# Gate/up tiles of four FFNs: all by seven block products, on operands taken from the residual stream without its reciprocal norm, and the biases of the second mixer prepared in the first

## The chip, the cores and the metric

One core of one Trainium2 chip runs the whole program. The metric is the device time of one execution in microseconds. TensorE (PE) multiplies, VectorE (DVE) and ScalarE (ACT) do the elementwise work, GpSimd (POOL) some more of it, and SyncE (SP) issues most transfers.

## The reference, cut to what matters

Two transformer blocks of two layers each run one after the other on 512 tokens (the second block adds 16 meta tokens, so 528) with 1024 features. Every layer is a mixer (four kinds, A to D) and then an FFN. What the change touches is the FFN:

```python
h = rmsnorm(x, norm_ffn[i])          # x * rsqrt(mean(x*x) + eps) * g
gu = h @ w_gate_up[i]                # 1024 -> 2 x 2816
x = x + (silu(gu[..., :D_FF]) * gu[..., D_FF:]) @ w_down[i]
```

In the second block the gate passes a causal convolution of width 3 over the tokens before the silu. The reciprocal norm is one number per token, so it can be multiplied in before the matrix product or after it.

## The kernel before, in words

Activations are kept transposed: X is eight tiles of 128 features by T tokens. Every float32 operand of a product is split into a high part, rounded to what one pass of TensorE takes, and the rest (`split`, L427: one ACT instruction, one DVE instruction), and each product is three matmuls (`mm3`, L253): hi by hi, hi by lo, lo by hi. So each weight tile costs ACT and DVE work as well as PE work.

A scheduler orders the instructions of each engine when the program is built; it follows the program's order but lets a later instruction go first where its inputs are there and an earlier one's are not. Buffers bound how far it runs ahead: 4 raw weight tiles, 4 `hi` and 4 `lo` tiles (`NRAW`, `NHI`), 3 PSUM banks for `mm`, 5 work tiles (`wk`), 60 slots.

**The norm** (`Norm`, L512) is spread over the mixer's output projection. When a tile X[k] is finished, `add` (L520) makes its operand xh, xl (L508 on ACT, L509 on DVE: X times the gain g, without the reciprocal norm) and adds its squares to `acc` (L533, L543). `sums` (L546) later reduces `acc` with small matmuls and a chain of 13 tiny DVE instructions, `rows` (L571) turns the result into a tile `rs` that holds the reciprocal norm of each token on all partitions.

**The FFN** (`ffn`, L982) runs over 22 tiles f of 128 gate and 128 up columns, in groups of 4, 2, 4, 4, 4, 4 (`GROUPS`). After a group, its share of the down product is left as a generator (`down`, L1028: eight tiles j, each added to X[j] on DVE at L687), and the next group's tiles draw on it: one down tile inside each gate/up tile (`between`), the rest behind it. During the first group there is no down work.

*Ordinary tiles*, f below 5 (`NPLAIN`): gate and up are each eight k-steps of three matmuls on xh, xl (`linT`, L266), 48 matmuls of 512 columns, or 96 of 264 with T of 528. The result is scaled by `rs` when it leaves PSUM (`scaled`, L402). Behind f = 0 to 3 stands the making of the block operands `xb` (L1024): X times gain times `rs` on DVE (`normed`, L992), then `Blocks.first` and `second` (L342, L353), with three subtractions on POOL and five splits for each of four pairs of tiles.

*Block tiles*, f from 5 on: `seven` (L294) loads the four blocks of the gate/up weights, makes four sums on DVE (L306 to L309) and splits all seven operands (three splits of 1024, one of 512). `blocks_to` (L379) computes gate and up by seven products (of 4 k-steps, 12 matmuls of 256 columns, 84 in all; 264 or 258 columns in the third and fourth FFN) and combines them with three ACT copies, three DVE additions and one more ACT copy (L400). No scaling: `xb` holds it already.

Behind either kind come the convolution (L977 on ACT, twice L980 on DVE; second block only), silu on ACT (L1022), gate times up (L1043) and its split (`ah`, `al`).

**The biases of mixer B** (`load_biases`, L1209) are prepared in the first FFN: POOL zeroes a scratch in DRAM and writes eight pieces into it (L1214, L1220), SP issues 16 DRAM-to-DRAM transfers (L1224), three at once and then one for each f from 4 on (`mid`), and at last 6 loads into SBUF and 5 of the memory keys and values (L1230, L897).

Of the kernel before, what the change touches and what calls it, by code (L numbers as in the profile page):

```python
# [9 lines left out]
F32 = mybir.dt.float32  # L10
# [24 lines left out]
NPLAIN = 5  # L35
XBAT = {0: (0,), 1: (1,), 2: (2,), 3: (3,)}
# [86 lines left out]
def kernel(ctx: ExitStack, tc: tile.TileContext, stop=None, **a):  # L123
# [170 lines left out]
    def seven(w, k0, nk, cols):  # L294
# [30 lines left out]
    class Blocks:  # L325


        def __init__(self, nk, o, n, tag, eng):
            self.n, self.o, self.tag, self.eng = n, o, tag, eng
            self.ops = {i: [None] * nk for i in range(1, 8)}  # L330
            self.raw = [None] * nk
# [7 lines left out]
        def win(self, z):  # L339
            return z[:, self.o:self.o + 2 * self.n].rearrange("p (i c) -> p i c", i=2)  # L340

        def first(self, k, z):  # L342

            h, l = slot(self.tag), slot(self.tag)
            v = self.win(z)
            split(self.part(h, 0), self.part(l, 0), v[:, 0, :])
            self.eng.tensor_tensor(v[:, 0, :], v[:, 1, :], v[:, 0, :], ALU.subtract)
            split(self.part(h, 1), self.part(l, 1), v[:, 0, :])
            for i, key in enumerate((1, 5)):
                self.ops[key][k] = self.part(h, i), self.part(l, i)  # L350
            self.raw[k] = v

        def second(self, k, z):  # L353

            v, t = self.win(z), self.raw[k]
            h, l = slot(self.tag), slot(self.tag)
            split(self.both(h), self.both(l), v)
            for i, key in enumerate((2, 3)):
                self.ops[key][k] = self.part(h, i), self.part(l, i)
            self.eng.tensor_tensor(t, v[:, 1, :].unsqueeze(1).to_broadcast([P, 2, self.n]), t, ALU.subtract)  # L360
            h, l = slot(self.tag), slot(self.tag)
            split(self.both(h), self.both(l), t)
            for i, key in enumerate((6, 7)):
                self.ops[key][k] = self.part(h, i), self.part(l, i)
            self.eng.tensor_tensor(v[:, 0, :], v[:, 0, :], t[:, 0, :], ALU.subtract)
            h = slot(self.tag)
            split(self.part(h, 0), self.part(h, 1), v[:, 0, :])
            self.ops[4][k] = self.part(h, 0), self.part(h, 1)
# [10 lines left out]
    def blocks_to(ws, bl, c1, c2, between):  # L379


        n = bl.n
# [16 lines left out]
        product(pa, 4, ws, bl, more=True)  # L399
        A.copy(c21, pa[:, :n])  # L400
# [111 lines left out]
    class Norm:  # L512
# [469 lines left out]
    def ffn(X, T, nj, wgu, wd, taps, done, lo=0, mid=None):  # L982

        xs = nj.xs
        lg = max(0, lo - 2)
        w = slice(lo, T)
        lb = max(0, lo - 4)
        xb = Blocks(4, lb, (T - lb) // 2, "xb", G)

        def normed(k, rs):  # L990
            z = wk("xn")
            V.scalar_tensor_tensor(z[:, :T], X[k][:, :T], gcol(nj.key, k), rs[:, :T], ALU.mult, ALU.mult)  # L992
            return z

        state = {}

        def up(f, put, between):
            c = f * P
            if mid is not None and f >= MID:
                next(mid, None)  # L1000
            gt, ut = wk("gt"), wk("ut")
            if f < NPLAIN:
                pcs = [wcols(wgu, 4 * h, [(c, P), (DFF + c, P)]) for h in range(2)]
                if f == 0:
                    hg, hu = Held(gt), Held(ut)
                    run(linT(pcs, 0, xs, T, hg.take, lo=lg, wide=True))
                    nj.sums()
                    run(linT(pcs, 1, xs, T, hu.take, lo=lo))
                    state["rs"] = nj.rows()
                    hg.scale(state["rs"])  # L1010
                    hu.scale(state["rs"])
# [26 lines left out]
        for gi, (f0, fn) in enumerate(GROUPS):  # L1038
# [39 lines left out]
    mnat = load_rows_of(a["mem"][0], NMEM)  # L1078


    def layer_a(X):
# [53 lines left out]
        class PairA(Pair):  # L1135
# [34 lines left out]
            def pv(self, b):  # L1170
# [3 lines left out]
                for u in range(u0, u1, P):  # L1174
# [8 lines left out]
        fill = Fill(q_tiles([6, 9, 7, 10], [3, 4]), q_tiles([2, 5, 8, 11], [2, 5]), memory_kv(),  # L1183
                    q_tiles([20, 21, 22, 23], [6, 7]))
# [6 lines left out]
    nf = Norm(S, ("norm_ffn", 0), "rsFA")  # L1191
# [15 lines left out]
    TB = []  # L1207

    def load_biases():  # L1209

        sc = dp.tile([P, 288], F32, name="rpbs")
        z = slot("zpad")[:, :288]
        G.memset(z, 0.0)
        G.dma_start(sc, z)  # L1214

        def scap(off, dims):
            return bass.AP(tensor=sc.tensor, offset=sc.offset + off, ap=dims)

        for r in range(8):
            G.dma_start(scap(r * 4608 + 8, [[384, 12], [48, 8], [1, 31]]), a["rpb_b"][0, :, 7 - r:15 - r, :])  # L1220

        td = dp.tile([P, 6 * 512], F32, name="TBd")
        for cc in range(16):
            nc.sync.dma_start(td[8 * cc:8 * cc + 8, :].rearrange("p (i j) -> p i j", j=32),  # L1224
                              scap(15 - cc, [[4608, 8], [48, 96], [1, 32]]))
            if cc > 1:
                yield
# [985 lines left out]
```

## Time and profile before

| | |
|---|---|
| runs | 2470.08, 2470.57, 2476.79 us; median 2470.57 |
| profiled execution | 2472.3 us, its span 2470.6 us |
| PE busy | 98% of the span |
| DVE, ACT, POOL busy | 73%, 48%, 9% |
| FFN gate/up of f = 0 to 4 begins at | 237.4, 814.6, 1524.2, 2106.3 us |

The profiled execution's time is its span and 1.7 us around it. Matmuls overlap, so the busy time of PE is no measure of its work: the distance from one start to the next is. A DVE instruction, too, is listed with a duration that overlaps the next one's by a little.

### The profile page before, as it was taken

The numbers are of one execution on the slowest core, as the hardware profiler recorded it, in microseconds if no ns is written. First come the engines' busy times: TensorE is split into PE (matmuls) and PEld (weight loads), VectorE is DVE, ScalarE is ACT, GpSimd is POOL, SyncE is SP. The second block draws the span as 40 slices with busy tenths as digits, with TensorE's granted clock in tenths as the row PEclk, the third lists the DMA queues.
The fourth block names the chain that finished last, engine by engine and source line by source line (L and its number), as shares of the span: only waits on it lengthen the run. The fifth ranks groups of instructions, "written<-read, shape, count | busy, mean of one in ns | idle before, by whom it ended". The sixth has DMA issues, their size and how long they took to land.

```text
span 2470.6 us, 44131 instructions
## 1 busy us (share of the span) xinstructions
PE 2428.9 (98%) x17446; PEld 2195.4 (89%) x17446; DVE 1812.7 (73%) x3531; ACT 1185.9 (48%) x2175; POOL 232.4 (9%) x359
## 2 busy tenths in 40 slices
PE   7999999999999999999999999999999999999999
PEld 6787789998887889998989999899999988989998
DVE  6875767777775778777766656888886775788885
ACT  4764435444565445445432233445444664445543
POOL 3120300003130100001011110200000000200000
PEclk9999999999999999999999999999999999999999
DMA  6152234444222223333411123123334222223332
GB/s 189 52 141 82 77 83 113 116 145 145 86 74 78 77 86 107 103 102 101 130 44 52 35 83 91 56 86 107 98 95 142 58 57 75 69 83 109 99 98 82
DMA packets 345443, 229.17 MB, mean 93 GB/s; under 512 B 54435, under 2 KB 335444, under 8 KB 345236
## 3 DMA queue, kind: packets, MB, share of 16 engines
q1 hardware_dynamic: 342212, 217.55, 30.0%
q0 software_dynamic: 2864, 8.77, 1.2%
q8 instruction: 137, 2.24, 0.4%
q14 instruction: 70, 0.57, 0.1%
q10 hardware_dynamic: 160, 0.04, 0.0%
HBM read 214.10 MB, written 13.74 MB: 92 GB/s over the span
## 4 chain that ended last, share of the span: by engine, by line
PE 83%; DVE 10%; issue 3%; ACT 2%; POOL 1%; SPq 1%; DMA 1%; DVEq 0%; ACTq 0%; POOLq 0%
PE mm L254 19%; PE mm L256 19%; PE mm L255 19%; PE pss L254 3%; PE pss L256 3%; PE pss L255 3%; DVE lo L430 2%; PE pso L254 1%; PE pso L256 1%; PE pso L255 1%; PE pss L847 1%; DVE xb L430 1%; PE pso L808 1%; PE pss L848 1%; PE pso L2045 1%
## 5 line engine op out<-in xcount | busy, mean ns | idle before, releaser
L429 ACT ACTIVATE hi<-raw 128x1024 fp32r<-128x1024 f32 (+1 forms) x454 | 470.7, 1039 | 520.5 <-PE pss L255 245.5
L430 DVE TENSOR_TENSOR lo<-raw,hi 128x1024 fp32r<-128x1024 f32 (+1 forms) x454 | 550.6, 1215 | 131.7 <-ACT hi L429 130.8
L254 PE MATMUL mm<-xh,hi 128*128 128x264 f32 (+3 forms) x1256 | 413.2, 329 | 8.0 <-ACT xh L508 2.4
L255 PE MATMUL mm<-xl,hi 128*128 128x264 f32 (+3 forms) x1256 | 405.3, 323 | 1.3 <-DVE xl L509 1.2
L256 PE MATMUL mm<-xh,lo 128*128 128x264 f32 (+3 forms) x1256 | 404.6, 323 | 0.0
L254 PE MATMUL mm<-ah,hi 128*128 128x512 f32 (+1 forms) x880 | 308.8, 352 | 7.5 <-DVE ut L404 4.9
L256 PE MATMUL mm<-xb,lo 128*128 128x256 f32 (+2 forms) x1088 | 308.1, 283 | 4.2 <-DVE lo L430 4.2
L255 PE MATMUL mm<-al,hi 128*128 128x512 f32 (+1 forms) x880 | 307.9, 350 | 0.1
L256 PE MATMUL mm<-ah,lo 128*128 128x512 f32 (+1 forms) x880 | 307.7, 350 | 0.0
L254 PE MATMUL mm<-xb,hi 128*128 128x256 f32 (+2 forms) x1088 | 307.3, 282 | 0.0
L255 PE MATMUL mm<-xb,hi 128*128 128x256 f32 (+2 forms) x1088 | 306.9, 282 | 0.0
L254 PEld LDWEIGHTS mm<-xh,hi 128*128 128x128 f32 x1256 | 238.8, 190 | 32.7 <-issue 6.7
L255 PEld LDWEIGHTS mm<-xl,hi 128*128 128x128 f32 x1256 | 238.9, 190 | 18.6 <-DVE xl L509 2.7
L256 PEld LDWEIGHTS mm<-xh,lo 128*128 128x128 f32 x1256 | 238.4, 190 | 18.4 <-issue 0.5
L687 DVE TENSOR_TENSOR xr<-mm,xr 128x512 f32<-128x512 f32 (+1 forms) x288 | 158.1, 558 | 124.1 <-PE mm L256 123.9
L256 PEld LDWEIGHTS mm<-xb,lo 128*128 128x128 f32 x1088 | 205.6, 189 | 5.1 <-DVE lo L430 5.0
L254 PEld LDWEIGHTS mm<-xb,hi 128*128 128x128 f32 x1088 | 205.5, 189 | 3.1 <-ACT hi L429 0.7
L255 PEld LDWEIGHTS mm<-xb,hi 128*128 128x128 f32 x1088 | 205.5, 189 | 2.2
L254 PEld LDWEIGHTS mm<-ah,hi 128*128 128x128 f32 x880 | 165.5, 188 | 29.8 <-DVE ut L404 6.6
L256 PEld LDWEIGHTS mm<-ah,lo 128*128 128x128 f32 x880 | 165.5, 188 | 22.7
L255 PEld LDWEIGHTS mm<-al,hi 128*128 128x128 f32 x880 | 165.5, 188 | 18.9 <-DVE al L430 1.1
L254 PE MATMUL pss<-xb,hi 128*128 128x256 f32 (+2 forms) x544 | 154.6, 284 | 0.0
(526 smaller groups left out, 5041.4 us busy)
## 6 DMA issues: line engine op xcount, KB each, us to landing
raw<-in_w_gate_up_dram SPq DMA_DIRECT2D x142, 256.0 KB, 3.0
raw<-in_ffn_w_up_dram SPq DMA_DIRECT2D x142, 256.0 KB, 3.0
raw<-in_w_down_dram SPq DMA_DIRECT2D x40, 512.0 KB, 3.4
raw<-in_ffn_w_down_dram SPq DMA_DIRECT2D x40, 512.0 KB, 3.4
raw<-in_mix_w_in_dram SPq DMA_DIRECT2D x28, 512.0 KB, 3.8
raw<-in_w_in_b_dram SPq DMA_DIRECT2D x20, 512.0 KB, 3.8
a<-in_w_gate_up_dram SPq DMA_DIRECT2D x34, 256.0 KB, 3.4
a<-in_ffn_w_up_dram SPq DMA_DIRECT2D x34, 256.0 KB, 2.9
```

The source lines that it names most:

```text
L254: PE.matmul(ps, r32(hi), r32(xh), start=first, stop=False, skip_group_check=more)
L255: PE.matmul(ps, r32(hi), r32(xl), start=False, stop=False, skip_group_check=more)
L256: PE.matmul(ps, r32(lo), r32(xh), start=False, stop=last, skip_group_check=more)
L429: A.activation(r32(dst_h), src, AF.Copy)
L430: V.tensor_tensor(r32(dst_l), src, dst_h, ALU.subtract)
L687: V.tensor_tensor(X[j][:, o:o + n], ps[:, :n], X[j][:, o:o + n], ALU.add)
L808: PE.matmul(po[64 * hh:64 * hh + 64, b * P:(b + 1) * P], self.vals(b, j, h), pt[:, (2 * hh + j) * P:(2 * hh + j + 1) * P], start=j == 0, s ...
L847: PE.matmul(ps[:, :n], r32(q), r32(k[0][:, k0:k0 + n]), start=True, stop=False)
L848: PE.matmul(ps[:, :n], r32(q), r32(k[1][:, k0:k0 + n]), start=False, stop=True)
L2045: PE.matmul(po[64 * hh:64 * hh + 64, b * P:(b + 1) * P], vt[b + j][:, kv * 64:kv * 64 + 64], PT[:, (2 * hh + j) * P:(2 * hh + j + 1) * P], ...
```

## The change

`NormB` replaces `Norm` for the four FFN norms: as each X[k] is finished in the mixer's output projection, it also makes the block operands, from X times gain without the reciprocal norm. Products 1, 2 and 3 use halves of xh, xl themselves; to make that possible, `seven` and `Blocks` now pair even with odd 128-row pieces of the contraction in place of the first four with the last four. All 22 tiles f are block tiles. `blocks_to` scales gate and up by `rs` on DVE: two more instructions and one that takes the place of the ACT copy. In f = 0 `sums` runs between products 2 and 6, and `rows` behind product 3. The biases go into the fill work of mixer A, in three pieces; their loads into SBUF are issued from POOL's queue behind the last gate/up tile of the first FFN.

```diff
-NPLAIN = 5
-XBAT = {0: (0,), 1: (1,), 2: (2,), 3: (3,)}
-    def seven(w, k0, nk, cols):
+    def seven(w, cols, nk=4):
...
-            r = (k0 + k * nk) * P
-            nc.sync.dma_start(chunks(t), w[r:r + nk * P, c:c + P].rearrange("(c p) n -> p c n", p=P))
+            nc.sync.dma_start(chunks(t), w[:, c:c + P].rearrange("(c i p) n -> i p c n", i=2, p=P)[k])
...
-        def first(self, k, z):
...
-        def second(self, k, z):
...
+        def even(self, k, x, g, xs):
+
+            self.ops[1][k] = self.half(xs, 0)
+            z = self.z = wk("xn")
+            A.activation(self.both(z), x[:, self.o:self.o + 2 * self.n].rearrange("p (i c) -> p i c", i=2), AF.Copy,
+                         scale=g)
+            z0, z1 = self.part(z, 0), self.part(z, 1)
+            V.tensor_tensor(z0, z1, z0, ALU.subtract)
+            h, l = self.t12 = slot("bt"), slot("bt")
+            split(self.part(h, 0), self.part(l, 0), z0)
+            self.ops[5][k] = self.part(h, 0), self.part(l, 0)
+
+        def odd(self, k, x, g, xs):
+
+            self.ops[2][k], self.ops[3][k] = self.half(xs, 0), self.half(xs, 1)
+            x1, x2 = self.half((x,), 0)[0], self.half((x,), 1)[0]
+            z = self.z
+            z0, z1 = self.part(z, 0), self.part(z, 1)
+            V.scalar_tensor_tensor(self.both(z), x2.unsqueeze(1).to_broadcast([P, 2, self.n]), g, self.both(z),
+                                   ALU.mult, ALU.subtract)
+            (h, l), (h2, l2) = self.t12, (slot("bt"), slot("bt"))
+            for i, (src, th, tl, j) in {6: (z0, h, l, 1), 7: (z1, h2, l2, 0), 4: (z0, h2, l2, 1)}.items():
+                if i == 4:
+                    V.scalar_tensor_tensor(z0, x1, g, z0, ALU.mult, ALU.subtract)
+                split(self.part(th, j), self.part(tl, j), src)
+                self.ops[i][k] = self.part(th, j), self.part(tl, j)
...
-    def blocks_to(ws, bl, c1, c2, between):
+    def blocks_to(ws, bl, c1, c2, rs, between, early=None, late=None):
...
         product(pd, 5, ws, bl)
+        product(pb, 2, ws, bl)
+        V.tensor_tensor(c11, pb[:, :n], p1, ALU.add)
+        if early:
+            early()
         product(pa, 6, ws, bl, more=True)
         A.copy(u2, pa[:, :n])
-        product(pb, 2, ws, bl)
-        V.tensor_tensor(c11, pb[:, :n], p1, ALU.add)
         product(pa, 7, ws, bl, more=True)
         A.copy(u3, pa[:, :n])
         V.tensor_tensor(c22, pd[:, :n], u3, ALU.add)
+        if rs is not None:
+            V.tensor_tensor(c22, c22, rs[:, w2], ALU.mult)
         between()
         product(pd, 3, ws, bl, more=True)
         V.tensor_tensor(c12, pd[:, :n], u2, ALU.add)
+        if late:
+            rs = late()
+            V.tensor_tensor(c22, c22, rs[:, w2], ALU.mult)
+        w = slice(bl.o, bl.o + 2 * n)
+        V.tensor_tensor(c1[:, w], c1[:, w], rs[:, w], ALU.mult)
         product(pa, 4, ws, bl, more=True)
-        A.copy(c21, pa[:, :n])
+        V.tensor_tensor(c21, pa[:, :n], rs[:, w1], ALU.mult)
+        return rs
...
+    class NormB(Norm):
...
+        def add(self, x):
+            k = len(self.xs)
+            Norm.add(self, x)
+            (self.bl.odd if k % 2 else self.bl.even)(k // 2, x, gcol(self.key, k), self.xs[k])
...
         def up(f, put, between):
...
-            else:
-                ws = seven(wgu, 0, 4, (c, DFF + c))
-                blocks_to(ws, xb, gt, ut, between)
+            ws = seven(wgu, (c, DFF + c))
+            state["rs"] = blocks_to(ws, xb, gt, ut, state["rs"], between, *(() if f else (nj.sums, nj.rows)))
...
-            for k in XBAT.get(f, ()):
-                xb.first(k, normed(k, state["rs"]))
-                xb.second(k, normed(k + 4, state["rs"]))
...
+        if mid is not None:
+            mid()
         run(before)
...
-        fill = Fill(q_tiles([6, 9, 7, 10], [3, 4]), q_tiles([2, 5, 8, 11], [2, 5]), memory_kv(),
-                    q_tiles([20, 21, 22, 23], [6, 7]))
+        fill = Fill(biases_out(), q_tiles([6, 9, 7, 10], [3, 4]), q_tiles([2, 5, 8, 11], [2, 5]),
+                    biases_columns(0, 8), memory_kv(), biases_columns(8, 16), q_tiles([20, 21, 22, 23], [6, 7]))
...
+    def biases_back():
         for hp in range(6):
             TB.append(slot("TB"))
-            nc.sync.dma_start(TB[hp][:, :512], td[:, hp * 512:(hp + 1) * 512])
-        memory_back()
+            G.dma_start(TB[hp][:, :512], rel["td"][:, hp * 512:(hp + 1) * 512])
+        memory_back(G)
```

`biases_out` holds the memset, the zeroing transfer and the eight writes of `load_biases` (POOL, unchanged), `biases_columns` the 16 transfers that SP issues, eight at a time. The four norms of the FFNs are now `NormB`.

## Rows read from the trace of the kernel before

**Rows 1.** The page: busy time, share and instructions of two engines; the chain by engine.
```profile
PE 2428.9 (98%) x17446; PEld 2195.4 (89%) x17446; DVE 1812.7 (73%) x3531; ACT 1185.9 (48%) x2175; POOL 232.4 (9%) x359
PE 83%; DVE 10%; issue 3%; ACT 2%; POOL 1%; SPq 1%; DMA 1%; DVEq 0%; ACTq 0%; POOLq 0%
```
**Rows 2.** Windows of ordinary tiles f = 1 to 4 and of five block products, FFN 1 to 4.
```profile
core 0: us, PE busy (x) PEld busy (x) DVE busy (x) ACT busy (x) POOL busy (x), PEclk, DMA share, GB/s
249.74:293.94 44.20, 44.20 (x195) 36.12 (x194) 36.73 (x52) 20.62 (x34) 12.15 (x10) 1.00 0.25 75
884.07:891.19 7.12, 7.12 (x61) 7.11 (x60) 4.98 (x9) 3.50 (x5) 0.00 (x0) 1.00 0.27 77
1538.30:1587.89 49.59, 47.65 (x386) 47.17 (x385) 45.73 (x70) 22.99 (x40) 13.77 (x11) 1.00 0.23 70
1603.66:1610.95 7.29, 7.29 (x62) 7.29 (x61) 4.00 (x7) 3.52 (x5) 0.00 (x0) 1.00 0.20 57
2119.91:2165.02 45.11, 45.11 (x290) 40.80 (x289) 41.13 (x60) 21.80 (x36) 13.62 (x9) 1.00 0.25 77
2178.45:2185.68 7.23, 7.23 (x61) 7.22 (x60) 5.98 (x9) 3.48 (x5) 0.00 (x0) 1.00 0.16 48
```
**Rows 3.** Windows of f = 6 to 9 in FFN 1 to 4.
```profile
327.92:387.17 59.25, 54.93 (x391) 51.20 (x389) 43.56 (x65) 28.04 (x46) 0.00 (x0) 0.97 0.34 92
905.07:956.42 51.35, 51.35 (x385) 48.55 (x384) 40.09 (x60) 26.52 (x43) 0.00 (x0) 1.00 0.33 98
1625.58:1678.22 52.64, 52.64 (x432) 52.34 (x431) 43.61 (x73) 27.48 (x45) 0.00 (x0) 1.00 0.32 96
2199.69:2251.45 51.76, 51.76 (x386) 49.48 (x384) 43.71 (x66) 28.42 (x46) 0.00 (x0) 1.00 0.33 98
```
**Rows 4.** FFN 1: a window inside f = 7; timeline of SP and of DVE (start, length).
```profile
340.00:352.00 12.00, 9.31 (x55) 8.29 (x55) 8.49 (x12) 5.91 (x10) 0.00 (x0) 0.86 0.31 88
...
307.45 3.74 SPq L1224 DMA_DIRECT2D TBd<-rpbs  x5
...
344.51 3.49 DVE L430 TENSOR_TENSOR lo<-raw,hi 128x1024 fp32r<-128x1024 f32 x3
```
**Rows 5.** DVE's group of one 256-column addition: count, busy us, mean ns.
```profile
L392 DVE TENSOR_TENSOR gt<-pso,u 128x256 f32<-128x256 f32 x34 | 14.4, 423 | 12.8 <-PE pso L256 12.7
```
**Rows 6.** Timeline of DVE, instructions one behind the other: start, length.
```profile
919.39 1.22 DVE L430 TENSOR_TENSOR lo<-raw,hi 128x1024 fp32r<-128x1024 f32 x1
920.52 0.69 DVE L430 TENSOR_TENSOR al<-ut,ah 128x512 fp32r<-128x512 f32 x1
921.13 0.68 DVE L430 TENSOR_TENSOR lo<-a,hi 128x512 fp32r<-128x512 f32 x1
...
1509.29 0.76 DVE L509 SCALAR_TENSOR_TENSOR xl<-xr,ncol,xh 128x528 fp32r<-128x528 f32 x1
1509.96 0.43 DVE L687 TENSOR_TENSOR xr<-mm,xr 128x264 f32<-128x264 f32 x1
1510.31 0.70 DVE L543 TENSOR_TENSOR acc<-acc,sq 128x528 f32<-128x528 f32 x1
```
**Rows 7.** Windows: the ends of mixers A, C and D, output projection alone.
```profile
204.00:237.40 33.40, 33.40 (x146) 27.14 (x145) 20.54 (x27) 14.76 (x20) 0.00 (x0) 1.00 0.32 94
1500.60:1524.25 23.65, 23.65 (x196) 23.65 (x195) 19.02 (x33) 12.82 (x18) 0.00 (x0) 1.00 0.31 90
2066.00:2106.20 40.20, 40.15 (x329) 39.95 (x328) 22.48 (x36) 16.36 (x22) 0.00 (x0) 1.00 0.30 87
```
**Rows 8.** DVE's timeline: first and last of the 14 instructions of the norm's chain.
```profile
243.96 0.16 DVE L457 TENSOR_SCALAR ms<-pss 128x4 f32<-128x4 f32 x1 [2.92 <-PE pss L454]
...
246.34 0.43 DVE L473 COPY rb<-rsFA 128x512 f32<-128x512 f32 x1
```
**Rows 9.** DMA issues of the biases (KB each, us to landing); a window of mixer A.
```profile
TBd<-rpbs SPq DMA_DIRECT2D x16, 96.0 KB, 3.1
...
90.00:150.00 60.00, 59.41 (x450) 48.69 (x449) 49.52 (x146) 45.33 (x120) 10.92 (x15) 1.00 0.17 54
```

More of the change, by code (lines that the diff above doesn't have):

```diff
@@ L325, with __init__, half @@
     class Blocks:
[L328 to L331, printed above, removed]
+        def __init__(self, o, n):
+            self.n, self.o = n, o
+            self.ops = {i: [None] * 4 for i in range(1, 8)}
+        def half(self, xs, i):
+            c = slice(self.o + i * self.n, self.o + (i + 1) * self.n)
+            return tuple(t[:, c] for t in xs)
         def part(self, t, i):
@@ L353, in second @@
-        def second(self, k, z):
[L355 to L368, printed above, removed]
+        def even(self, k, x, g, xs):
[8 more added lines that the diff above has]
+            self.ops[5][k] = self.part(h, 0), self.part(l, 0)
@@ L980, in conv, with ffn @@
             V.scalar_tensor_tensor(out[:, o:T], src[:, o - d:T - d], taps[n - 1 - d], out[:, o:T], ALU.mult, ALU.add)
-    def ffn(X, T, nj, wgu, wd, taps, done, lo=0, mid=None):
-        xs = nj.xs
-        lg = max(0, lo - 2)
+    def ffn(X, T, nj, wgu, wd, taps, done, mid=None, lo=0):
         w = slice(lo, T)
[L987 to L995, printed above, removed]
+        xb = nj.bl
+        state = {"rs": None}
         def up(f, put, between):
             c = f * P
-            if mid is not None and f >= MID:
-                next(mid, None)
             gt, ut = wk("gt"), wk("ut")
[L1002 to L1011, printed above, removed]
-                else:
-                    run(linT(pcs, 0, xs, T, lambda out: scaled(out, state["rs"], gt), lo=lg))
-                    run(linT(pcs, 1, xs, T, lambda out: scaled(out, state["rs"], ut), lo=lo))
-            else:
-                ws = seven(wgu, 0, 4, (c, DFF + c))
-                blocks_to(ws, xb, gt, ut, between)
+            ws = seven(wgu, (c, DFF + c))
+            state["rs"] = blocks_to(ws, xb, gt, ut, state["rs"], between, *(() if f else (nj.sums, nj.rows)))
             if taps is not None:
@@ L1078, with scap, biases_out, biases_columns @@
     mnat = load_rows_of(a["mem"][0], NMEM)
+    TB, rel = [], {}
+    def scap(off, dims):
+        return bass.AP(tensor=rel["sc"].tensor, offset=rel["sc"].offset + off, ap=dims)
+    def biases_out():
+        rel["sc"] = dp.tile([P, 288], F32, name="rpbs")
+        z = slot("zpad")[:, :288]
+        G.memset(z, 0.0)
+        G.dma_start(rel["sc"], z)
+        for r in range(8):
+            G.dma_start(scap(r * 4608 + 8, [[384, 12], [48, 8], [1, 31]]), a["rpb_b"][0, :, 7 - r:15 - r, :])
+        yield 0.1
+    def biases_columns(lo, hi):
+        if lo == 0:
+            rel["td"] = dp.tile([P, 6 * 512], F32, name="TBd")
+        for cc in range(lo, hi):
+            nc.sync.dma_start(rel["td"][8 * cc:8 * cc + 8, :].rearrange("p (i j) -> p i j", j=32),
+                              scap(15 - cc, [[4608, 8], [48, 96], [1, 32]]))
+        yield 0.1
     def layer_a(X):
@@ L1205, in to_cols @@
         lag.put(XB[j])
[L1207 to L1227, printed above, removed]
+    def biases_back():
         for hp in range(6):
             TB.append(slot("TB"))
-            nc.sync.dma_start(TB[hp][:, :512], td[:, hp * 512:(hp + 1) * 512])
-        memory_back()
+            G.dma_start(TB[hp][:, :512], rel["td"][:, hp * 512:(hp + 1) * 512])
+        memory_back(G)
     nb = Norm(S, ("norm_mix", 1), "rsB")
     lag = Lag(nb, NLAG)
-    ffn(X, S, nf, a["w_gate_up"][0], a["w_down"][0], None, to_cols, mid=load_biases())
+    ffn(X, S, nf, a["w_gate_up"][0], a["w_down"][0], None, to_cols, biases_back)
     lag.end()
```

30 lines of the change are left out of this document (12 added, 18 removed).

## Prediction

> **What bounds the kernel now.** I read the page first: PE is busy 98% of the span and holds 83% of the chain that ended last, DVE 10% of it at 73% busy [rows 1]. So a matmul less is time gained, as long as DVE keeps up, and the question is where it does not. The table by windows answers that for the stretches the change touches. Ordinary tiles run at 44.20/4 = 11.05 us each in FFN 1, block products at 7.12/5 = 1.42 us, so 9.97 us for seven [rows 2]; in both PE has no idle time. In f = 6 to 9, FFN 2 takes 51.35 us with no idle PE, and FFN 1 takes 59.25 us for the same instructions, with PE busy 54.93 us and a granted clock of 0.97 [rows 3]. What FFN 1 has there and FFN 2 has not are the bias transfers. The timelines show how they act: SP issues five in a row at 307.45, behind them the weight loads come in clumps, and DVE then does three weight splits in one piece of 3.49 us while PE waits; in these 12 us PE works 9.31 us and the clock is 0.86 [rows 4].
>
> **What it removes, on PE.** Five f per FFN turn from ordinary to block. FFN 1 and 2: 11.05 - 9.97 = 1.08 us each, 5.4 us per FFN. FFN 3: of 49.59 us 47.65 are busy, so 11.91 us each, against 7 x 7.29/5 = 10.21; 1.70 x 5 = 8.5 us. FFN 4: 45.11/4 = 11.28 against 7 x 7.23/5 = 10.12; 5.8 us [rows 2]. Together **25.1 us**. The matmuls of `sums` and `rows` stay; they only stand elsewhere.
>
> **The biases leave FFN 1.** If its f = 6 to 9 then run as FFN 2's, **7.9 us** go [rows 3]. In mixer A they meet DMA engines that are 17% busy and transfers that land in 3.1 us [rows 9]. POOL has nine issues more there at a time when it works 10.9 of 60 us; behind them on POOL stand only score biases that are made pairs ahead. SP has 16 more, with weight loads behind them; those loads are issued one set of tiles ahead, so a burst of eight should be covered. If that cover is gone, mixer A could clump as FFN 1 did: bounds -1 (order alone) to 7.9 us, and I take 1, near the covered end, because of the idle DMA engines. The 11 loads back into SBUF move from SP to POOL, behind the last gate/up tile of FFN 1; they are needed only by mixer B's biases, after its first projections, and I cost them at nothing. What stands behind them on POOL are the small copies that begin mixer B, which are used after whole products. Were those late by all 11 issues it would be a few microseconds; that lies within the bounds just given.
>
> **What it adds on DVE.** One instruction's price is the distance to the next start: 1.13 us for a split of 1024, 0.61 for 512 columns, 0.67 for a scalar_tensor_tensor, 0.35 for 256 [rows 6]; 256 columns with one input in PSUM are listed at 0.42 [rows 5], as long as the 264 of the spacing row. A block tile without down work is then: four sums 2.4, splits 3 x 1.13 + 0.6 = 4.0, three combinations 1.05, the new scaling 0.35 + 0.61 + 0.35 = 1.3, gate times up and its split 1.2; **9.95 us against PE's 9.97**. In FFN 3 and 4 the convolution adds 2 x 0.67: 11.3 against 10.2 and 10.1. So in the first group, which has no down work, DVE is level with PE in two FFNs and behind it in two. ACT loses one copy per tile and is no bound. POOL's three subtractions per pair go, and with them the 16 `xn` tiles.
>
> The block operands cost, for each pair of X tiles, on DVE 2 x 0.35 in `even` and 0.67 + 4 x 0.35 in `odd`: 2.8 us, 11 us per mixer. Mixer A's end has DVE busy 20.5 of 33.4 us, mixer D's 22.5 of 40.2: there it fits. Mixer C's has 19.0 of 23.65 [rows 7], because its last half has only four k-steps per tile. Three of four pairs fall before its end, 8.4 us, and the four sums of the first gate/up tile 2.4: 29.8 us into 23.65. Of the 6 us that do not fit I carry 5 over, since the four sums can be made earlier.
>
> The first group, from the end of the mixer to the last product of f = 3, on DVE: the last X tile (residual, xl, squares, `odd`) 4; the norm's chain 2.8 [rows 8]; the last weight split of f = 0 0.6; f = 1 to 3's weights 3 x 6.4 = 19.2; f = 0 to 2's combining, scaling and split 3 x 3.55 = 10.7; f = 3's combining 1. That is 38.3 us, against four block tiles and 1.2 us of norm matmuls on PE, 41.1 us. FFN 1 and 2: DVE 93% busy. FFN 4: 38.3 + 3 x 1.35 + 0.5 (wider norm) = 42.9 against 42.2, level. FFN 3: 42.9 and a backlog of 5 from mixer C, 48 against 42.7.
>
> How much PE loses when DVE is nearly full is not in the sums, since it depends on order. The nearest rows: FFN 3's ordinary tiles, DVE 45.73 of 49.59, lost PE 1.94 us [rows 2]; FFN 1's f = 6 to 9 lost 7.9 with DVE at 74% [rows 3]; FFN 4's f = 1 to 4, DVE 41.13 of 45.11, lost nothing [rows 2]. So 0 to 7.9 for an FFN; I take 3 in FFN 1 and 2, nearest to the row with DVE equally full, 4 in FFN 4, and in FFN 3 the 5.3 us by which DVE is behind and 3 more: **18 us given back** (bounds 5 and 37).
>
> Later f carry the scaling too, 1.3 us each. In f = 6 to 9 DVE goes from 40.1 to 45.3 of 51.35 in FFN 2, to 48.8 of 52.64 in FFN 3 and to 48.9 of 51.76 in FFN 4 [rows 3]; from f = 10 on a tile has more down work and PE more time. Also, the last quarter leaves PSUM on DVE in place of ACT, where it queues behind weight splits, and the silu and the down product wait for it. I take 0.5, 0.5, 2 and 1.5 for f = 6 to 9 and 1.5 for all the rest: **6 us** (bounds 0 and 31.6, four times what FFN 1 lost).
>
> **The sum**: -25.1 - 7.9 + 1 + 18 + 6 = **-8.0 us** from 2472.3, the profiled execution's own time (span 2470.6 and 1.7 around it): 2464.3. The median of the runs is 1.7 lower than that execution, so against it I predict **2462.5 us**.
>
> **Rivals.** *DVE eats all of it* (chance 0.18). The give-back in the first groups is 25 and not 18: what PE gains, DVE costs, and what is left is the biases less the later f: -25.1 - 7.9 + 1 + 25 + 6 = -1, so 2469.6. For it: 9.95 against 9.97, and PE's order in f = 0, where the norm's matmuls stand between products 2 and 6 and wait for the last squares. Against it: FFN 4's ordinary tiles at 91% without loss.
>
> *The waits cost clock as well* (0.10). In the 12 us of [rows 4] the clock was 0.86, a loss of 12 x 0.14 = 1.7 us beside the idle time. One such stretch in each first group is 6.7 us: 2464.3 + 6.7 - 1.7 = 2469.3. Against it: FFN 3's stretch with 1.94 us of idle kept a clock of 1.00 [rows 2], so it takes a longer single wait, as behind mixer C. By that rule the trace agrees: the Trainium skill ("TensorE: Matmul & The Clock Gate", "HAM oscillation — how this bites in real kernels") has PE throttle to half rate after idle time and pay to warm up again.
>
> *PE gets everything* (0.12). The scheduler fills DVE's gaps, as in FFN 4's 91%; only 2 us are given back: -25.1 - 7.9 + 2 = -31, so 2439.6. Against it: FFN 3, where DVE's work exceeds PE's whatever the order.
>
> *Slower: the splits clump in every FFN* (0.20). Place: f = 6 to 9, where half-size down products leave 12.8 us per f. Price: FFN 1's 7.9 us, four times, in place of the 6 above: -25.1 - 7.9 + 1 + 18 + 31.6 = +17.6, so 2488.2. It decides once DVE's slack per f, 2.8 us in FFN 2 today, is about 1 us or less; in FFN 3 and 4 it will be that. For it: FFN 1 clumped with more slack. Against it: there the loads were late, not DVE.
>
> **How the numbers follow.** A measurement of this kernel tells 0.3%, 7.4 us, from no change. My forecast has 0.40; of that 0.35 is faster by over 0.3% and 0.05 within it. With *PE gets everything*, faster is 0.47; with the two that end near 2469.5, same is 0.33; slower 0.20. Since both signs hold much, the forecast's own range is 2454 to 2466 (10 to 22 us given back in the first groups in place of 18). The whole range reaches down into *PE gets everything*, to 2446, and up to 2484, half-way into the clumping case.
>
> **What the profile would show.** Ordinary gate/up matmuls (xh, 512 columns) gone from the FFNs and 84 of 256 in their place at 1.42 us per product. FFN 1's f = 6 to 9 near 52 us, with a clock of 1.00. In the first groups, DVE over 90% busy and PE idle for 2 to 4 us in FFN 1, 2 and 4 and for about 8 in FFN 3, most of it just behind mixer C. Mixer A unchanged within 2 us. I am wrong if FFN 1's f = 6 to 9 stay above 55 us, if PE waits for weight splits in f = 6 to 9 of the others, or if the first groups lose under 1 us or over 8 each.

## The result, and the profile after

The changed kernel takes 2488.26 us (median of four runs, 2484.76 to 2493.65) against 2472.22 us of the kernel before on the same chip: a ratio of **1.0065, 95% interval 1.0046 to 1.0083**. It is slower by 16 us, where I had forecast 8 us less. The profiled executions are 2493.65 and 2472.3 us, 21.3 us apart, and that difference is what the table shares out (the profiled execution of the changed kernel is the slowest of its four runs, so this distance is 5 us more than that of the medians). A mixer ends with the last matmul of its output projection, an FFN with the last of its down products.

| us | before | after | | | before | after |
|---|---|---|---|---|---|---|
| mixer A | 237.2 | 255.1 | | FFN 1 | 357.8 | 352.1 |
| mixer B | 219.3 | 222.0 | | FFN 2 | 350.2 | 351.6 |
| mixer C | 359.5 | 359.1 | | FFN 3 | 371.8 | 376.7 |
| mixer D | 210.2 | 211.9 | | FFN 4 | 358.5 | 357.2 |

So mixer A lost 17.9 us, and four FFNs that should have gained 25 us of matmuls and 8 us of bias clump gained 0.7 between them. (The differences of mixers C and D are within what they show from profile to profile over all the kernels of this study: C 353.6 to 361.2, D 208.1 to 213.8 us. Mixer B takes 219.0 to 221.2 in the others, so its 222.0 is at most 0.8 us beyond that.)

The page of the changed kernel, the rows that answer to [rows 1]:

```profile
PE 2431.5 (98%) x17806; PEld 2201.2 (88%) x17806; DVE 1965.9 (79%) x3923; ACT 1214.3 (49%) x2201; POOL 170.5 (7%) x322
PE 87%; DVE 6%; ACT 3%; issue 3%; SPq 1%; DMA 1%; POOL 0%; DVEq 0%; ACTq 0%; POOLq 0%
```

DVE works 153 us more, as it had to. But its share of the chain fell from 10% to 6%: what came up is PE, from 83% to 87%, and ACT, from 2% to 3%. That is the first hint that DVE, on which the whole prediction turned, isn't where the time went.

**Mixer A.** A window of the changed kernel in mixer A, with the columns' names:

```profile
core 0: us, PE busy (x) PEld busy (x) DVE busy (x) ACT busy (x) POOL busy (x), PEclk, DMA share, GB/s
150.00:180.00 30.00, 17.45 (x112) 15.48 (x113) 11.69 (x15) 7.79 (x11) 3.85 (x8) 0.77 0.61 147
```

Here 12.5 us of 30 are idle, and the mean granted clock falls to 0.77. SP's timeline (start, length of the run of issues) shows what came before:

```profile
110.17 0.51 SPq L1097 DMA_DIRECT2D TBd<-rpbs  x1
157.29 3.05 SPq L907 DMA_DIRECT2D memd<-memk  x4
163.16 0.32 SPq L907 DMA_DIRECT2D memd<-memv  x1
163.53 4.91 SPq L1097 DMA_DIRECT2D TBd<-rpbs  x7
168.48 1.19 SPq L211 DMA_DIRECT2D raw<-in_w_in_a_dram  x2
```

and PE's timeline shows its only long wait there:

```profile
174.44 0.79 PE L252 MATMUL mm<-xh,hi 128*128 128x512 f32 x1 [11.84 <-ACT hi L437]
```

SP issues nothing from 110.7 to 157.3 us: the next thing in its queue is a store of the memory keys (L907), which waits for POOL's copies of them (L862). Behind it stand the last value store, seven bias columns, and only then the weights of the last query tiles, for which PE stops. In the kernel before, those weights were issued ahead of the stores:

```profile
128.08 2.98 SPq L213 DMA_DIRECT2D raw<-in_w_in_a_dram  x2
```

**The FFNs.** f = 6 to 9 of FFN 1 to 4, which answer to [rows 3]:

```profile
344.33:396.23 51.90, 51.90 (x385) 48.29 (x384) 43.05 (x70) 24.00 (x38) 0.00 (x0) 1.00 0.33 97
918.63:970.58 51.95, 51.84 (x386) 48.24 (x384) 43.09 (x70) 23.84 (x38) 0.00 (x0) 1.00 0.33 97
1641.42:1695.67 54.25, 54.07 (x435) 53.01 (x433) 47.89 (x84) 27.19 (x42) 0.00 (x0) 1.00 0.31 91
2218.44:2270.70 52.26, 52.26 (x386) 49.01 (x385) 46.17 (x75) 25.95 (x41) 0.00 (x0) 1.00 0.31 92
```

FFN 1's clump is gone, 59.25 to 51.90 us. The others got a little longer, without the idle time that a clump of late splits would show. One tile far inside FFN 2 has the same, first before, then after:

```profile
1049.35:1064.89 15.54, 15.54 (x110) 14.47 (x108) 11.60 (x17) 7.19 (x12) 0.00 (x0) 1.00 0.34 101
```
```profile
1049.11:1064.80 15.69, 15.69 (x109) 14.35 (x108) 12.86 (x20) 6.94 (x11) 0.00 (x0) 1.00 0.35 101
```

0.15 us for the same matmuls, with PE listed as fully busy. Where it goes is seen only instruction by instruction. After, PE (last matmul of product 6, two k-steps of a down tile, first two of product 7) and ACT:

```profile
1070.34 0.28 PE L254 MATMUL mm<-bt,lo 128*128 128x256 f32 x1
1070.46 0.40 PE L252 MATMUL mm<-ah,hi 128*128 128x512 f32 x1
...
1071.62 0.39 PE L254 MATMUL mm<-ah,lo 128*128 128x512 f32 x1
1071.96 0.39 PE L252 MATMUL mm<-bt,hi 128*128 128x256 f32 x1
1072.18 0.28 PE L253 MATMUL mm<-bt,hi 128*128 128x256 f32 x1
...
1070.59 1.06 ACT L437 ACTIVATE hi<-raw 128x1024 fp32r<-128x1024 f32 x1 [1.76 <-PE mm L253]
1071.55 0.35 ACT L392 COPY u<-mm 128x256 f32<-128x256 f32 x1
```

Product 7 accumulates in the same PSUM bank `pa` as product 6, so it may not begin before ACT has copied product 6 out (`u2`, L392). In the kernel before, product 2 stood between the two. The change moves product 2 ahead of product 6; the scheduler now puts down k-steps there as cover, but ACT takes a weight cast of 1.06 us first, and the copy ends as product 7 starts: PE begins it 0.34 us after the matmul ahead of it, whose 512 columns elsewhere take 0.23, and its second matmul starts 0.22 us later, where the matmuls of 256 columns around it are 0.12 apart. The view of one line says how often, for the copy L392 of the changed kernel (who waited for it: us, times):

```profile
L392 ACT COPY u<-mm x88: 351/357/397, 261.4 to 2451.9; 128x256 f32<-128x256 f32 x44, 128x264 f32<-128x264 f32 x22, 128x258 f32<-128x258 f32 x22
...
  PEld mm L252: 28.7, 79
  PE mm L252: 4.8, 10
```

79 of 88 tiles have the weight load of product 7 waiting for it. In the kernel before, nothing waited for the same copy.

**FFN 3's start** is the one place where PE waits long for DVE. Windows of the changed kernel; then its timeline, with the 3.2-us wait on PE and what DVE does until then:

```profile
1530.00:1545.00 15.00, 14.05 (x111) 13.42 (x109) 15.00 (x34) 11.75 (x24) 0.00 (x0) 1.00 0.01 4
1545.00:1560.00 15.00, 11.24 (x67) 10.16 (x68) 11.88 (x26) 4.77 (x9) 0.00 (x0) 0.77 0.18 53
```
```profile
1549.03 0.59 PE L254 MATMUL pso<-xh,lo 128*128 128x264 f32 x1 [3.21 <-DVE lo L438]
...
1547.35 0.49 DVE L363 SCALAR_TENSOR_TENSOR xn<-xr,ncol,xn 128x264 f32<-128x264 f32 x1
1547.75 1.22 DVE L438 TENSOR_TENSOR lo<-raw,hi 128x1024 fp32r<-128x1024 f32 x1
```

DVE is busy 15.00 of 15 us, still making block operands (L363) 7 us after mixer C's last matmul, and the weight split for product 2 comes behind them.

### The profile page after: what moved, and what is told of

Its sections match the earlier page's. It is cut to its first block, busy times and chain, and to the rows that moved or that the text cites. A ratio compares the mean times of both kernels' runs of the same rounds, so it can differ in the third digit from the quotient of the medians.

```text
span 2491.9 us, 45467 instructions
## 1 busy us (share of the span) xinstructions
PE 2431.5 (98%) x17806; PEld 2201.2 (88%) x17806; DVE 1965.9 (79%) x3923; ACT 1214.3 (49%) x2201; POOL 170.5 (7%) x322
## 4 chain that ended last, share of the span: by engine, by line
PE 87%; DVE 6%; ACT 3%; issue 3%; SPq 1%; DMA 1%; POOL 0%; DVEq 0%; ACTq 0%; POOLq 0%
PE mm L252 20%; PE mm L253 19%; PE mm L254 19%; PE pss L252 3%; PE pss L253 3%; PE pss L254 3%; PE pso L254 2%; PE pso L252 2%; PE pso L253 2%; PE pss L868 1%; DVE lo L438 1%; ACT hi L437 1%; PE pso L829 1%; PE pss L869 1%; PE pso L2046 1%
## 5 line engine op out<-in xcount | busy, mean ns | idle before, releaser
L437 ACT ACTIVATE hi<-raw 128x1024 fp32r<-128x1024 f32 (+1 forms) x474 | 491.9, 1042 | 540.3 <-PE pss L253 245.4
L438 DVE TENSOR_TENSOR lo<-raw,hi 128x1024 fp32r<-128x1024 f32 (+1 forms) x474 | 569.2, 1202 | 103.2 <-ACT hi L437 101.0
L252 PE MATMUL mm<-xh,hi 128*128 128x264 f32 (+3 forms) x1168 | 367.3, 315 | 22.0 <-ACT hi L437 16.2
L253 PE MATMUL mm<-xl,hi 128*128 128x264 f32 (+3 forms) x1168 | 360.4, 309 | 1.4 <-DVE xl L517 1.2
L254 PE MATMUL mm<-xh,lo 128*128 128x264 f32 (+3 forms) x1168 | 359.4, 308 | 1.0 <-DVE lo L438 0.9
L252 PE MATMUL mm<-bt,hi 128*128 128x256 f32 (+2 forms) x1056 | 308.8, 292 | 6.1 <-ACT u L392 4.8
L253 PE MATMUL mm<-bt,hi 128*128 128x256 f32 (+2 forms) x1056 | 298.7, 283 | 0.0
L254 PE MATMUL mm<-bt,lo 128*128 128x256 f32 (+2 forms) x1056 | 298.6, 283 | 0.0
L252 PEld LDWEIGHTS mm<-bt,hi 128*128 128x128 f32 x1056 | 199.4, 189 | 34.9 <-ACT u L392 28.7
L254 PEld LDWEIGHTS mm<-bt,lo 128*128 128x128 f32 x1056 | 200.0, 189 | 0.0
L253 PEld LDWEIGHTS mm<-bt,hi 128*128 128x128 f32 x1056 | 199.8, 189 | 0.1
L254 PE MATMUL pso<-xh,lo 128*128 128x256 f32 (+2 forms) x352 | 100.0, 284 | 3.2 <-DVE lo L438 3.2
```

Source lines behind the costliest of these rows:

```text
L252: PE.matmul(ps, r32(hi), r32(xh), start=first, stop=False, skip_group_check=more)
L253: PE.matmul(ps, r32(hi), r32(xl), start=False, stop=False, skip_group_check=more)
L254: PE.matmul(ps, r32(lo), r32(xh), start=False, stop=last, skip_group_check=more)
L437: A.activation(r32(dst_h), src, AF.Copy)
L438: V.tensor_tensor(r32(dst_l), src, dst_h, ALU.subtract)
```

## The experiments

My theories after the result: (1) the order of products 6 and 7 on one bank costs the FFNs their gain; (2) the order on SP's queue costs mixer A; (3) DVE's scaling is nearly hidden; (4) DVE is behind only at the end of mixer C. The rival to all four is the reason I had forecast with: DVE is full, and what waits for it spreads.

**One edit to the products (e1).**

```diff
         product(pd, 5, ws, bl)
-        product(pb, 2, ws, bl)
-        V.tensor_tensor(c11, pb[:, :n], p1, ALU.add)
         if early:
+            product(pb, 2, ws, bl)
+            V.tensor_tensor(c11, pb[:, :n], p1, ALU.add)
             early()
         product(pa, 6, ws, bl, more=True)
         A.copy(u2, pa[:, :n])
+        if not early:
+            product(pb, 2, ws, bl)
+            V.tensor_tensor(c11, pb[:, :n], p1, ALU.add)
         product(pa, 7, ws, bl, more=True)
```

> The changed kernel with one edit: for f > 0 product 2 stands between products 6 and 7 again. Theory 1 (products 6 and 7 share one PSUM bank and stand back to back, so PE waits for ACT's copy of product 6 before product 7 may start): the waits at the head of a product on mm from bt, 6.8 + 6.9 + 11.0 + 6.0 = 30.7 us over the four FFNs in the trace of after, mostly go: 18 to 28 us less than the changed kernel, near 2465. Rival (the FFNs are slow because DVE carries the scaling and the operands): the waits move to other instructions, under 4 us less, near 2486. Mixer A stays at 253 to 255 us in either.

Measured: 2464.82 us, 0.9956 of the kernel before (0.9943 to 0.9969); 23.4 us less than the changed kernel by the medians, 27 by the two ratios. The FFNs take 346.8, 345.4, 372.7 and 353.5 us, 19.2 us less together, and mixer A still 254.2. Who waits for the copy now:

```profile
  PEld mm L252: 2.4, 5
  PE mm L252: 1.2, 3
```

Five waits where there were 79. Theory 1 holds.

**The same order in the kernel before (e5)**: products 2 and 6 exchanged there, nothing else.

> The kernel before with one edit: in its block tiles (f from 5 on, 17 per FFN, 68 in all) product 2 stands ahead of product 6. Theory 1 (the copy of product 6 is all that is between two products on one bank): by the 23.4 us that 84 tiles gave back when the order was restored, 0.28 us each, 68 tiles cost 12 to 20 us: 1.005 to 1.008 of the kernel before. Rival (that wait only appears since DVE carries more per tile in the changed kernel): within 3 us of the kernel before.

Measured: 2486.2 us, ratio 1.0053 (1.0041 to 1.0066), 13 us slower by the ratio. Its view of the copy:

```profile
L392 ACT COPY u<-mm x68: 351/358/383, 314.3 to 2442.8; 128x256 f32<-128x256 f32 x34, 128x264 f32<-128x264 f32 x17, 128x258 f32<-128x258 f32 x17
...
  PEld mm L254: 17.7, 67
```

67 of its 68 block tiles have the weight load wait, and a tile of FFN 2 takes 15.65 us in place of 15.50. Here DVE has its old load, so the order alone is enough. And by e1 it takes no other edit to be rid of it. The Trainium skill ("Perfetto Trace Analysis", "Matmuls") has a rule that fits: independent groups of matmuls should rotate through different PSUM banks, so that the copy of one runs beside the next group. The runs agree; products 6 and 7 share a bank because they accumulate, and product 2 is the independent group between them.

**SP's queue (e2, e3).** e2 lets the query weights go first; e3 leaves the order and takes the stores off SP:

```diff
-  biases_columns(0, 8), memory_kv(), biases_columns(8, 16), q_tiles([20, 21, 22, 23], [6, 7]))
+  biases_columns(0, 8), memory_kv(), q_tiles([20, 21, 22, 23], [6, 7]), biases_columns(8, 16))
```
```diff
-                    nc.sync.dma_start(d[i * P:(i + 1) * P, :], t[:, :512])
+                    G.dma_start(d[i * P:(i + 1) * P, :], t[:, :512])
```

> The changed kernel with one edit: the second half of the bias columns stands behind mixer A's last query tiles in place of ahead of them, so SP issues their weights ahead of the stores of the memory keys, as in the kernel before. Theory 2 (those two weight loads stood on SP behind a store that waits for POOL's copies, and PE waited 12 us for them): mixer A falls from 255 to 238 to 241 us, 13 to 17 us less in all, near 2473. Rival (the bias transfers themselves, by their traffic or by POOL's nine issues, hold mixer A up): mixer A stays above 250 us, under 4 us less.

> The changed kernel with one edit: the five stores of the memory keys and values are issued from POOL's queue, behind the copies that they wait for; all the bias columns still stand on SP ahead of the last query weights. Theory 2a (it is the waiting stores that hold SP): mixer A falls to 238 to 242 us as when the weights go first. Rival 2b (it is the run of seven bias transfers, 4.9 us of issue on SP): mixer A falls by under 4 us, or not at all.

Measured: e2 2474.56 us, ratio 1.0000 (0.9989 to 1.0011), mixer A 243.3; e3 2473.87 us, ratio 0.9996 (0.9987 to 1.0006), mixer A 241.6. First SP in e2, then SP in e3:

```profile
150.55 1.50 SPq L211 DMA_DIRECT2D raw<-in_w_in_a_dram  x2
152.10 1.21 SPq L1097 DMA_DIRECT2D TBd<-rpbs  x1
159.05 3.66 SPq L907 DMA_DIRECT2D memd<-memk  x4
```
```profile
109.51 6.48 SPq L1097 DMA_DIRECT2D TBd<-rpbs  x8
150.68 1.51 SPq L211 DMA_DIRECT2D raw<-in_w_in_a_dram  x2
```

Either way the weights leave 18 us earlier than the 168.48 of the changed kernel, and the window 150 to 180 us has PE busy 28.99 us (e2) and 28.24 (e3) of 30, with a granted clock of 1.00. In e3 eight columns still stand ahead of the weights, and it makes no difference: it was the waiting stores, not the run of bias transfers. The Trainium skill ("DMA: Bandwidth & Descriptors", "Issuing engines are not separate DMA queues") says that issuing from several engines saves only the sequencer's time to start a transfer, usually little. Here the five issues take 3.4 us of SP's time in the changed kernel, and moving them took 13.5 us from mixer A: what an issue waits for counts as well, and the measurement decides. Mixer A came down by 12 and 13.5 us: e2 ends 2 us above what I had expected, e3 inside it.

**The bias part alone on the kernel before (e6).**

> The kernel before with one part of the change alone: the biases are prepared in mixer A, in the changed kernel's places, and loaded back behind the last gate/up tile of FFN 1. Theory 2: SP gets the same order as in the changed kernel, so mixer A grows by 13 to 18 us; FFN 1's f = 6 to 9 lose their clump, 6 to 8 us; together 5 to 12 us slower than before. Rival (in mixer A the cost came from the block operands that are made at its end): mixer A stays within 3 us, and the kernel is 4 to 8 us faster.

Measured: 2486.04 us, ratio 1.0048 (1.0034 to 1.0062). Mixer A takes 254.1 us, with the same queue and the same wait:

```profile
156.15 3.06 SPq L886 DMA_DIRECT2D memd<-memk  x4
...
162.39 4.91 SPq L1101 DMA_DIRECT2D TBd<-rpbs  x7
167.35 1.19 SPq L213 DMA_DIRECT2D raw<-in_w_in_a_dram  x2
...
173.14 0.80 PE L254 MATMUL mm<-xh,hi 128*128 128x512 f32 x1 [11.68 <-ACT hi L429]
```

The block operands, which this kernel doesn't make in mixer A, have no part in its 17 us. FFN 1 gained 4.0 us (357.8 to 353.8), and would have gained 7 but for one wait of 3 us in f = 18, where a weight load landed late. Such a wait on PE, of 1.7 to 2.9 us and in that tile, stands in the profiles of e6, e7, e9 and e10 and in none of the others. What stands beside it are the loads of the biases back into SBUF: they come behind the last gate/up tile in the program, but POOL issues the first of them as early as f = 17 or 18. First DVE and POOL in e9, then POOL in e4:

```profile
510.63 0.69 DVE L306 TENSOR_TENSOR raw<-raw 128x512 f32<-128x512 f32 x1 [4.21 <-DMA raw<-in_w_gate_up_dram]
...
499.27 2.66 POOL L1239 DMA_DIRECT2D TB<-TBd  x5 [59.10 <-PE mm L254]
501.92 1.60 POOL L921 DMA_DIRECT2D memb<-memd  x3
```
```profile
504.22 1.62 POOL L1234 DMA_DIRECT2D TB<-TBd  x3 [330.75 <-PE mm L254]
```

Eight go out at once in e6, e9 and e10 and four in e7; every other kernel that loads back from POOL issues three there, the rest later. The weight load that DVE then waits for lands after 7.9 to 8.4 us with eight of them beside it and after 4.8 to 6.7 with three or four (where its landing is recorded), against 2.9 for a load just before. So the loads back are what delays it, as far as the traces go; no run moved them alone.

**Both edits (e4).** e1's and e2's.

> The changed kernel with both edits: product 2 between 6 and 7 for f > 0, and the second half of the bias columns behind mixer A's last query tiles. If theories 1 and 2 both hold and their costs lie on the path one after the other, they add up: 31 to 45 us less than the changed kernel, 2443 to 2457, 15 to 29 under the kernel before. If DVE is the bound behind them, the sum falls short: 2465 to 2475.

Measured: **2455.2 us, ratio 0.9918 (0.9904 to 0.9932)**. In the stages the two gains add up: mixer A 243.5 us (11.6 less than the changed kernel), the FFNs 345.4, 345.3, 372.6 and 354.3 (20.0 less). DVE, at 80% of the span, doesn't stand behind them as the next bound.

**Without the scaling (e7).** e4 without its multiplications by `rs`, and the last quarter on ACT.

> The changed kernel with both edits, and without the scaling of gate and up by the reciprocal norm: no multiplications by rs, and the last quarter leaves PSUM by an ACT copy again (that part of the computation is left out). It takes some 1.3 us of DVE per tile away. Theory 3 (with the products' order restored, DVE's scaling is nearly hidden): 0 to 4 us less than with both edits. Rival (DVE is the bound that the prediction feared): 8 us less or more. In either, FFN 3's wait of 3.7 us near 1552 us stays if it comes from the operands made in mixer C, and goes if it comes from the scaling.

Measured: 2455.43 us, ratio 0.9924 (0.9911 to 0.9937): no different from e4. Its page:

```profile
PE 2409.5 (98%) x17806; PEld 2199.5 (90%) x17806; DVE 1855.5 (76%) x3659; ACT 1237.1 (50%) x2289; POOL 170.9 (7%) x322
```

DVE works 110 us less than in e4 (1965.1), ACT, which takes over the last quarter, 14 more (1223.1 in e4), and the kernel isn't faster. Within this total FFN 3 and 4 fell by 5.2 and 3.5 us; the wait near 1552 us went, so that one did come from the scaling or from the last quarter on DVE, which this edit takes away together. FFN 1, FFN 2 and mixer C rose by 4.7, 1.1 and 6.2: 1.9 of FFN 1's is the late load and 2.4 are two waits for ACT in its first 21 us (1.59 and 0.80), which e4 hasn't, and mixer C's is within its spread. So theory 3 holds for the kernel as a whole, and FFN 1 and 2 gain nothing; in FFN 3 and 4 this work on DVE cost 8.7 us, which the total hides behind what the other stages pay.

**The operands in mixer C (e11).** e4, with products 7 and 4 of that FFN given product 6's operand.

> The changed kernel with both edits, and in mixer C alone the operands of products 7 and 4 aren't made (product 6's operand stands for them; that part of the computation is left out). It takes 1.1 us of DVE per pair of X tiles away, 4.4 us in all, at mixer C's end. Theory 4 (DVE is behind there, and the weight splits of FFN 3's first tile queue behind the operands): the wait of 3.4 us at product 2 of f = 0 falls under 1 us, its granted clock of 0.77 returns to over 0.9, and FFN 3 falls from 372.6 by 3 to 7 us. Rival (that wait comes from a late weight load): it stays, FFN 3 within 2 us.

Measured: 2450.72 us, ratio 0.9907 (0.9886 to 0.9927); FFN 3 takes 367.1 us, 5.5 less. The same 15 us behind mixer C, first in e4, then here:

```profile
1514.00:1529.00 15.00, 11.24 (x66) 10.16 (x67) 11.85 (x26) 4.79 (x9) 0.00 (x0) 0.77 0.19 54
```
```profile
1514.00:1529.00 15.00, 14.52 (x113) 13.80 (x113) 14.23 (x32) 7.00 (x12) 0.00 (x0) 1.00 0.22 63
```

4.4 us of DVE work taken away, and the wait with its low clock is gone. Theory 4 holds for this wait. Its "only" does not: the second wait of FFN 3, 3.3 us near 1553 us, is still there, on a weight split of DVE, and it is the one that went in e7.

**Where the biases could stand.** e8 is e1's and e3's edits, e12 all three.

> The changed kernel with product 2 between 6 and 7 and with the memory stores on POOL's queue (in place of the later bias columns). Theories 1 and 2a: as with both edits, 2450 to 2458; mixer A at 238 to 243 us, without the wait of 2.5 us at 195 us that the later bias columns left in front of the output weights. Rival: POOL's queue delays something and mixer A is above 246.

> The changed kernel with product 2 between 6 and 7 for f > 0, the later bias columns behind mixer A's last query tiles, and the memory stores on POOL's queue. Theory 2: neither the wait of 1.4 us at 162 us (bias columns ahead of the query weights) nor the 2.5 us at 195 us (bias columns behind the waiting stores, ahead of the output weights) is left: mixer A 238 to 241 us, 2448 to 2455. Rival: one of them stays, mixer A at 242 to 244, as with both edits.

Measured: e8 2458.32 us, ratio 0.9941 (0.9928 to 0.9954), mixer A 241.1; e12 2453.08 us, ratio 0.9917 (0.9898 to 0.9936), mixer A 244.0. In mixer A, e12 went against its expectation. The bias columns go out early, and the wait ahead of the output weights stays:

```profile
151.24 1.50 SPq L211 DMA_DIRECT2D raw<-in_w_in_a_dram  x2
152.79 8.14 SPq L1100 DMA_DIRECT2D TBd<-rpbs  x8
161.03 51.25 SPq L211 DMA_DIRECT2D raw<-in_w_out_dram  x36
...
198.87 0.50 PE L252 MATMUL mm<-oh,hi 128*128 128x512 f32 x1 [1.64 <-ACT hi L440]
```

So it isn't made by SP. It stands in every kernel in which the query tiles go ahead of the columns. The traces show a little more: in e4 and e12 this matmul is the first of the output projection, and ACT casts no weights for the 37 us and more before (from 159 to 197.8 us in e12), though SP issued the output weights from 161 us on; in the kernel before and in e8 the projection's first matmuls stand at 169.7 and 174.6 us, between the attention's. So PE waits for the first cast of a projection that starts late; why it is put that late stays open.

e9 and e10 put the biases back behind mixer A, on POOL's and on SP's queue:

```diff
-  fill = Fill(biases_out(), ..., biases_columns(0, 8), memory_kv(), biases_columns(8, 16), ...)
+  fill = Fill(..., memory_kv(), ...)
...
+            if mid is not None and f >= 2:
+                next(mid, None)
...
     def biases_back():
+        yield from biases_out()
+        for cc in range(16):
+            yield from biases_columns(cc, cc + 1)
```

> The changed kernel with product 2 between 6 and 7 for f > 0, and with the biases back behind mixer A, but all 16 bias columns issued from POOL, which has nothing else to do there, so nothing of them stands on SP. Theory 2c (bias transfers cost only by what stands behind them on SP): mixer A 237 to 240 us, FFN 1 344 to 347 us (345.4 with both edits), 2445 to 2452. Rival (16 small transfers in a row cost by their traffic, whatever the queue): mixer A's end or FFN 1 loses 5 us or more, 2454 or above.

> The same with the 16 bias columns on SP, among the weight loads of FFN 1, three at once and then one per f from f = 2 on. Theory 2c: mixer A 237 to 240 us as in the run beside it, and FFN 1 pays on SP what it paid in the kernel before, 3 to 8 us more than 345.4, so 2450 to 2458. Rival: FFN 1 stays at 344 to 347, since here each tile has block operands and SP has time.

Measured: e9 2452.13 us, ratio 0.9909 (0.989 to 0.9928), mixer A 237.9, FFN 1 349.1; e10 2453.44 us, ratio 0.9919 (0.99 to 0.9937), mixer A 237.9, FFN 1 352.2. First POOL in e9, then SP and PE in e10:

```profile
244.64 10.29 POOL L1102 DMA_DIRECT2D TBd<-rpbs  x15 [3.04 <-DMA rpbs<-in_rpb_b_dram]
```
```profile
280.82 2.35 SPq L1102 DMA_DIRECT2D TBd<-rpbs  x3
283.28 4.63 SPq L301 DMA_DIRECT2D raw<-in_w_gate_up_dram  x3
...
305.74 0.38 PE L252 MATMUL mm<-xh,hi 128*128 128x256 f32 x1 [2.61 <-ACT hi L440]
```

Against 345.4 in e4, FFN 1 is 3.7 us longer with fifteen transfers in a row on POOL's queue, 2.2 of it the late load of f = 18, and 6.8 us longer with them among SP's weight loads, 1.9 of it that load. FFN 1 of e9 misses the 344 to 347 that I expected. The late load goes with the loads back, which both have, so 1.5 us is left for the bias transfers as traffic and 4.9 where weights stand behind them: theory 2c holds for the larger part. Mixer A without the biases is 237.9 us, so in their best place there (241.1, e8, with the stores on POOL) they cost 3 us. Mixer A and FFN 1 together are 588.9 in e4, 587.2 in e8, 587.0 in e9 and 590.1 in e10: mended, it makes no difference that can be told where the biases are prepared.

## Why the prediction was wrong

Its own terms against the profiled executions. The sum was -8.0, the measured difference +21.3.

| term | forecast | measured |
|---|---|---|
| five f per FFN to block | -25.1 | (not separable; taken as forecast) |
| biases leave f = 6 to 9 of FFN 1 | -7.9 | -7.4 (59.25 to 51.90) |
| biases in mixer A | +1 | +17.9 |
| given back in the FFNs, first groups and later f | +24 (18 + 6) | +31.8 |
| mixers B to D and the end | 0 | +4.1, noise |

The FFN row is what is left: together they changed by -0.7, and -25.1 - 7.4 + 31.8 = -0.7. With the products in their old order (e4) they changed by -20.7, so 12 us are given back, 9 of them in FFN 3.

**The step that failed first: "a burst of eight should be covered".** I looked at the transfers that the change adds, at DMA engines 17% busy and at loads one set ahead, and took 1 us with bounds of -1 and 7.9. I didn't write down what stands on SP ahead of the added transfers. The memory stores stand there, 46.6 us from one issue to the next in the changed kernel, and the seven columns behind them kept the query weights from going ahead as they did before. Traffic and length of the burst are at most 3.7 of the 17.9 us (e3, which keeps both: 241.6 against 237.9 without the biases in e9), so the bounds, taken from the burst in FFN 1, didn't hold it.

**The second: I priced the order of the products at nothing.** The prediction names that the norm's matmuls stand between products 2 and 6 in f = 0, and looks at f = 0 alone. That product 2 had been the cover for the copy between products 6 and 7, in every tile, I didn't see; the price is 19 to 20 us over the four FFNs (e1, e4), about 0.23 us for each of the 84 tiles that those edits change.

**The third: DVE was priced too high where it is only level with PE.** "How much PE loses when DVE is nearly full" was put at 18 us in the first groups and 6 later. With the order restored all of it is 12 us. In FFN 1, 2 and 4, where I had put 3, 3 and 4 and a share of the 6, it was 0.4, 0.5 and 1.6. The estimate of FFN 3 was good, number and mechanism: 5.3 us behind, 3 more and 2 in f = 6 to 9; there 9.3 us went (e4), and 5.5 come back without mixer C's operands (e11), 5.2 without the scaling and the last quarter (e7).

**The rivals.** 2488.2 of the slower one is the measured time, but its mechanism isn't what happened: f = 6 to 9 take 51.90 to 54.25 us, and PE doesn't wait for splits there. The clock came down where PE waited long, as the rival of the clock has it: 0.77 in 15 us around the wait of 3.21 us, 0.77 in 30 around 11.84 (each the mean of stretches at full and at half clock). By that the trace agrees with the Trainium skill ("TensorE: Matmul & The Clock Gate", "HAM oscillation — how this bites in real kernels"), by which idle PE is throttled and has to warm up again. That it takes a longer single wait, as the prediction infers, is not borne out: 15 us around a wait of 2.89 us in e6 kept 1.00, and 15 us around one of 1.64 us in e4 had 0.89. The short waits of theory 1 cost no clock: 1.00 in all four windows of f = 6 to 9.

Right were the matmuls that go, the clump that goes and the size of FFN 3's backlog. That the 11 loads back into SBUF cost nothing is right for the changed kernel and for mixer B (219.0 to 219.4 us in e1 to e3, which have them, 219.3 before), but not in general: they go with the late weight load of f = 18, 1.7 to 2.9 us on PE in e6, e7, e9 and e10.

## What to carry to other kernels

Before pricing a transfer that is added to an in-order queue, list what stands ahead of it and behind it and when each can start: a store that waits for compute closes the queue for everything after it, so loads that feed the critical engine go ahead of it or the store goes to another queue. Before moving a group of matmuls, ask which evacuation it was covering: two groups on one PSUM bank need something between them that is longer than the copy and whatever the copying engine does first. And a busy engine's share of the span prices nothing by itself: with the order restored DVE at 80% cost 9 us in FFN 3 and under 2 in each of the others, and only work taken away stage by stage told which.

## What the runs showed that I had not expected

Waits of a few tenths that the listed busy time hides were worth 20 us, since they came 79 times: PE shows 15.69 of 15.69 us busy in the tile that lost 0.15, and only the idle time of the weight loads (28.7 us for one copy, 2.4 with the order restored) gives it away. After such a wait the second matmul of 256 columns starts 0.22 us behind the first in place of 0.12.

The scheduler's own repair, down k-steps between products 6 and 7, nearly covers the copy (0.35 us) but not the weight cast (1.06 us) that ACT takes ahead of it in some two thirds of the tiles.

What stands last in the program isn't last in time: the loads back, written behind the last gate/up tile, went out among the weight loads of f = 18, three, four or eight at once.
